# A second level of block products for one of the seven products, in the first feed-forward weights of a streaming encoder layer on one Trainium2 core

## The chip, the cores and the metric

The kernel runs on one core of a Trainium2 chip. The metric is the device time of one execution in microseconds (us), the median of several runs. In the profile the engines are PE (TensorE, matmuls; PEld are its weight loads), DVE (VectorE), ACT (ScalarE), POOL (GpSimd) and SP (SyncE, which only issues transfers; SPq is its queue). All arithmetic is of single precision.

## The reference, cut to what matters

One encoder layer is computed for 1024 new frames and for 64 frames of a second stream, so 1088 rows of 1024 features. It has a half-step feed-forward, attention of two kinds, and a second half-step feed-forward, with a layer norm after each of the three.

```python
def _swiglu(x, wi, wo):
    a, u = jnp.split(x @ wi, 2, axis=-1)
    return (jax.nn.silu(a) * u) @ wo

def _layer(x, mixer, ...):
    h = _layer_norm(alpha * x + 0.5 * _swiglu(x, ffn1_wi, ffn1_wo), ln1_g, ln1_b)
    ...                                  # attention and its projections: mix
    h = _layer_norm(alpha * h + mix, ln2_g, ln2_b)
    h = _layer_norm(alpha * h + 0.5 * _swiglu(h, ffn2_wi, ffn2_wo), ln3_g, ln3_b)
```

`wi` is 1024 x 5632 (a gate half and a linear half of 2816 columns), `wo` is 2816 x 1024. The change concerns `x @ wi` in both feed-forwards.

## The kernel before, in words

**Tiles.** Features lie on the 128 partitions: the residual is eight tiles `y0` to `y7` of 128 features x 1088 columns (`NT`). The 2816 hidden features are 22 tiles (`NF`) of 128, numbered f. A matmul is exact enough only if each factor is split into an upper part (rounded to the format that TensorE takes at full rate) and a lower part (the rest), so each product of 128 x 128 by 128 x 272 (`SUB` = 272, a quarter of the columns) is three matmuls: upper by upper, upper by lower, lower by upper.

**Block products.** With the residual cut into halves of its features and halves of its 1088 columns, A11, A12, A21, A22, a tile's product with `wi` is four blocks by four, and Winograd's scheme makes it from seven block products instead of eight, P1 to P7. Each takes one factor of the residual (A11, A12, A22, or a sum S1 to S4 of blocks, each four row blocks deep) and one block of the weights or a difference of blocks. P1 and P2 are A11 and A12 by the fetched blocks b11 and b21; P6, P5, P3, P7, P4 follow. One product is 2 column parts x 4 row blocks x 3 = 24 matmuls, done by `product`, L921. `after`, L955, moves the results: the first sum of a bank is copied by ACT into a line c (`copy`), later ones are added by DVE (`plus`), then come the silu on ACT and the product of the gate and the linear half on DVE (`times`), whose result is stored in `ff_d` for tiles below 18. There are three lines, c, c21 and c22, used by every tile in turn.

**Order.** `add_ffn7` writes the whole order of a feed-forward (L1371 to 1386): tiles 0 and 1 by plain products (`plain`), tiles 2 and 3 side by side, tiles 4 to 19 singly, one product after the other in the order P1, P2, P6, P5, P3, P7, P4, then tiles 20 and 21 side by side, then the second feed-forward weights. `sums_of_weights`, L1125, stands after P1 of tiles 4 to 12: it fetches four blocks of `wo`, makes four differences of 512 columns on DVE (tiles st) and stores them for later.

**Weights.** Six raw slots of 512 columns (`fetch`, L818; named wr, more and q in the trace) take the fetched blocks. Four slots (w_s) hold a product's split weights. `prepare`, L841, takes the next product's unit when a slot is handed back by `done_with`: a split is one copy of 512 columns on ACT and one difference on DVE; P6 makes four differences of 512 columns first. A planner (`Plan`) places each task in the order of its engine's instructions while the program is written; what engine it is and where it stands is fixed then. In these stages the weights' upper parts are ACT's and the lower parts DVE's, and POOL has nothing to do.

**Around it.** `put_factors`, L715, adds the bias to the normed residual and splits it into A11 to A22 before the second feed-forward. A chain of steps that builds attention bias tables runs beside the first feed-forward's tile loop.

Of the kernel before, what the change touches and what calls it, by code (L numbers as in the profile page):

```python
# [32 lines left out]
P = 128  # L33
# [101 lines left out]
class Plan:  # L135
# [93 lines left out]
    def count(self, e, op, outs, ins, args, kw):  # L229
        dma = op == "dma_start"  # L230
        kept = [x for x in outs if x.space != bass.MemoryType.DRAM or x.tensor.name.startswith(("ff_", "tw_"))]
# [117 lines left out]
def tile_trunk(ctx, tc, a):  # L349
# [34 lines left out]
    o_d = dram.tile([D, NT], F32, name="o_d")  # L384
    bt_d = [dram.tile([P, HEADS * 256], F32, name=f"bt_d{i}") for i in range(2)]
# [329 lines left out]
    def put_factors(G):  # L715

        def put(k, b, y, bias, t0):
            n = TB[b]
            t1 = plan.task(biased(n), f"ln_w{b}", lambda e: plus_bias(e, y[:, :n], bias), [t0], 3)
# [82 lines left out]

    def add_ffn7(wi, wo, wl, G, gi, put, beside_it, last, end):
# [9 lines left out]
        sums_of, made, outs, banks, touched, back = {}, {}, {}, {}, set(), set()  # L813
# [27 lines left out]
        def prepare():  # L841
# [7 lines left out]
            def task(engines, queue, fn, deps, keys=(), reads=()):  # L849
                return plan.task(engines, queue, fn, deps, 1, lambda: all((n, f) in src for n in keys),  # L850
                                 lambda: [x() for x in reads], when)
# [4 lines left out]
            def parts(x, deps, more=(), keys=(), done=None):  # L856
                hi = w[:, 0]

                def copy(e):
                    if e == "act":  # L860
                        nc.scalar.activation(hi, x(), AF.Copy)
                    else:
                        nc.vector.tensor_copy(hi, x())

                def rest(e):
                    of(e).tensor_tensor(w[:, 1], x(), hi.bitcast(F32), op=OP.subtract)
# [3 lines left out]
                t1 = task((("act", 93 + 0.84 * 512), ("dve", WH * (69 + 0.52 * 512)))[alone], "w_h", copy, deps, keys,  # L870
                          [x] if keys else [])
                u.t = low[u.kind, f] = task((("dve", 69 + 1.04 * 512), ("pool", WP * (146 + 2.1 * 512)))[alone], "w_l", rest,
                                            [t1] + list(more))
            if u.kind[0] == "q":
# [5 lines left out]
            elif u.kind == "P6":  # L880
# [3 lines left out]
                m4 = low["t4", f] = task(shared(512), "w_t", minus(b21, b21, b22), [m2, low["P2", f]])  # L884
# [4 lines left out]
            elif u.kind == "P3":  # L889
                parts(part("b22x", f), [], keys=["b22x"], done="b22x")  # L890
            elif u.kind == "P7":
# [29 lines left out]
        def product(f, kind):  # L921
            u = get_unit(kind, f)
            w, factor = u.slot, FACTOR[kind]
            if kind == "P1":
                F[f] = Bag()
                F[f].f, F[f].h, F[f].t, F[f].a, F[f].b = f, G.h(f), {}, {}, {}
            o = F[f]
            h, t = o.h, o.t
            second = f in SECONDS
            base = 4 if second else 0  # L930
            for s in range(2):
                in_b = kind in ("P2", "P7", "P4")
                if kind == "P1":
                    o.a[s] = take_bank(base + s)
                elif kind == "P2":
                    o.b[s] = take_bank(base + 2 + s)
                else:
                    wait(t[{"P6": "r1", "P5": "r2", "P3": "r4", "P7": "c11", "P4": "c22"}[kind], s])
                p = (o.b if in_b else o.a)[s][:, :SUB]
                for k in range(4):  # L940
                    x, c = G.xc[factor][:, k, :, s * SUB:(s + 1) * SUB], slice(k * P, (k + 1) * P)
                    wait(*G.ready[factor, k])
                    first, final = k == 0 and kind in ("P1", "P2", "P7"), k == 3
                    nc.tensor.matmul(p, w[:, 0, c], x[:, 0], start=first, stop=False, skip_group_check=True)
                    nc.tensor.matmul(p, w[:, 0, c], x[:, 1], start=False, stop=False, skip_group_check=True)
                    nc.tensor.matmul(p, w[:, 1, c], x[:, 0], start=False, stop=final, skip_group_check=True)
                    tick()
                if not (second and kind in ("P1", "P2")):
                    after(f, kind, s, p, base)
                if kind == "P7" and f + 1 in SECONDS:  # L950
                    after(f + 1, "P1", s, F[f + 1].a[s][:, :SUB], 4)
                    after(f + 1, "P2", s, F[f + 1].b[s][:, :SUB], 4)
            done_with(u)

        def after(f, kind, s, p, base):  # L955
# [3 lines left out]
            c, c21, c22 = (x[:, s] for x in G.t)  # L959
# [18 lines left out]
            if kind == "P1":  # L978
# [8 lines left out]
            elif kind == "P3":  # L987
# [3 lines left out]
                G.user[0, s] = [t["h1", s]]  # L991
# [10 lines left out]
        def plain(f, half):  # L1002

            if f not in F:
                F[f] = Bag()
                F[f].f, F[f].h, F[f].t = f, G.h(f), {}
# [89 lines left out]
        def early():  # L1096
# [3 lines left out]
            wait(*G.sums_made)  # L1100
            roles.update(mm=[0, 1, 2, 3])
# [274 lines left out]
        for f in range(EIGHT + 2, NF - 2):  # L1376
# [11 lines left out]
        for x, fs in order:  # L1388
            for f in fs:
                if x == "plain":  # L1390
# [4 lines left out]
                    steps.append(lambda f=f, half=half: plain(f, half))  # L1395
                elif x == "beside":
# [41 lines left out]
    HT, SUB = NT // 2, NT // 4  # L1438
    EIGHT = 2
# [12 lines left out]
    G1.y = [yp.tile([P, NT], F32, name=f"y{d}") for d in range(KT)]  # L1452
# [94 lines left out]
    def bias_tables():  # L1547
# [7 lines left out]
        for i in range(2):  # L1555
# [13 lines left out]
            for h in range(HEADS):  # L1569
# [4 lines left out]
                yield later("pe", 9000)  # L1574
# [17 lines left out]
    def after_plain1(f, half):  # L1592
# [7 lines left out]
        if (f, half) == (1, 1):  # L1600
            for _, third in G1.made:
                third()

    G1.after_plain = after_plain1
# [873 lines left out]
    def to_out():  # L2478
# [5 lines left out]
        G2.y = [yp.tile([P, NT], F32, name=f"y2_{d}") for d in range(KT)]  # L2484
# [57 lines left out]
    def after_plain2(f, half):  # L2542
# [9 lines left out]
        if (f, half) == (1, 1):  # L2552
            for _, third in G2.made:
                third()

# [13 lines left out]
    G2.to_second = to_second2  # L2569
# [147 lines left out]
```

## Time and profile before

| | us |
|---|---|
| median of 3 runs | 2436.49 (2435.34 to 2437.27) |
| the profiled execution's own time | 2433.65 |
| its span in the trace | 2431.9 |
| tile loop of pairs, first feed-forward | about 98.6 to 445.7 |
| tile loop of pairs, second feed-forward | about 1795.4 to 2130.9 |

The profile is one page of one execution and a trace that can be queried. A row of the page's fifth part, and of the view by groups, names line, engine, operation, result<-operands and shapes, and then the busy time, the mean duration in ns of one, and the idle time of that engine just before, with what ended it. The helper that records operations makes nearly every row's line L124, so the names tell operations apart: b is a bank of sums, w_s the split weights, wr, more and q the raw weights, A and S the factors, c a line. The table by windows gives for each stretch its length, the busy time (and number of instructions) of PE, PEld, DVE, ACT and POOL, the clock that TensorE was granted, the share of the DMA engines and GB/s. A row of the waits gives engine and what it waited for, the total in us, the number of waits and the longest. A row of the timeline gives start, duration, engine, operation and, in brackets, the idle time before it and what ended that.

### The profile page before, as it was taken

Reading aid. Unit: us, or ns where it says so; the run is one execution under the profiler, and the core shown is the slowest. Engines: PE = TensorE matmul, PEld = TensorE weight load, DVE = VectorE, ACT = ScalarE, POOL = GpSimd, SP = SyncE. Lnnn points to the kernel's source line nnn. Section 1 sums busy time; section 2 is a strip of 40 time slices with the busy share of each in tenths; the row PEclk is TensorE's granted clock in tenths of the full one; section 3 lists DMA queues with packets and bytes.
Section 4 is the critical chain, followed back from the end, with each engine's and each line's share of the span. In section 5 each row is a group of like instructions: output and inputs, shape, how many; then the busy total and the mean of one; then the engine's idle time right before and its main releaser. Section 6 shows DMA issues by size and latency. Waiting matters only on the chain.

```text
span 2431.9 us, 46878 instructions
## 1 busy us (share of the span) xinstructions
PE 2406.8 (99%) x17339; PEld 2363.8 (97%) x17340; DVE 1744.2 (72%) x4248; ACT 1307.8 (54%) x2771; POOL 312.3 (13%) x443
## 2 busy tenths in 40 slices
PE   9999999999999999999999999999999999999998
PEld 9999999999999999999999999999999999999997
DVE  7666655667876889898776677669956665576786
ACT  6333333344435698788866777445643333443344
POOL 0000000000014223222253342211000000000000
PEclk9999999999999999999999999999999999999999
DMA  5476532264223322223221112565256653236323
GB/s 189 128 212 203 175 103 88 66 215 144 85 88 114 119 80 75 93 79 93 85 82 57 57 42 73 172 195 173 82 149 186 188 155 93 80 103 211 109 83 100
DMA packets 228213, 293.29 MB, mean 121 GB/s; under 512 B 21056, under 2 KB 151472, under 8 KB 227952
## 3 DMA queue, kind: packets, MB, share of 16 engines
q1 hardware_dynamic: 221936, 283.38, 37.8%
q10 hardware_dynamic: 5488, 4.70, 0.8%
q8 instruction: 136, 2.23, 0.4%
q0 software_dynamic: 560, 2.21, 0.2%
q14 instruction: 93, 0.76, 0.1%
HBM read 215.48 MB, written 75.00 MB: 119 GB/s over the span
## 4 chain that ended last, share of the span: by engine, by line
PE 86%; DVE 7%; ACT 2%; DMA 2%; issue 1%; SPq 0%; POOL 0%; DVEq 0%; ACTq 0%; POOLq 0%
PE b L124 86%; DVE w L124 1%; DVE y L124 1%; DVE scores L124 1%; ACT scores L124 1%; SPq L124 0%; DVE w_s L124 0%; DVE pt L124 0%; DMA st<-in_wo_dram 0%; ACT w L124 0%; DVE k L124 0%; DVE sc L124 0%; ACT w_s L124 0%; DVE junk L124 0%; DMA x<-o_d 0%
## 5 line engine op out<-in xcount | busy, mean ns | idle before, releaser
L124 PE MATMUL b<-x,w_s 128*128 128x384 f32 (+1 forms) x3528 | 636.3, 332 | 3.4 <-ACT w_s L124 2.5
L124 PE MATMUL b<-A,w_s 128*128 128x272 f32 (+2 forms) x4848 | 634.4, 290 | 3.2 <-ACT rstd L124 0.9
L124 PEld LDWEIGHTS b<-A,w_s 128*128 128x128 f32 x4848 | 619.4, 188 | 7.9 <-DVE A L124 1.6
L124 PEld LDWEIGHTS b<-x,w_s 128*128 128x128 f32 x3528 | 584.8, 188 | 10.8 <-ACT w_s L124 3.2
L124 PE MATMUL b<-S,w_s 128*128 128x272 f32 x4032 | 516.0, 288 | 2.2 <-ACT c L124 2.2
L124 PEld LDWEIGHTS b<-S,w_s 128*128 128x128 f32 x4032 | 508.2, 188 | 5.2 <-ACT c L124 3.5
L124 ACT ACTIVATE w_s<-wr 128x512 fp32r<-128x512 f32 (+1 forms) x373 | 252.4, 678 | 368.4 <-PE b L124 201.6
L124 DVE TENSOR_TENSOR w_s<-wr,w_s 128x512 fp32r<-128x512 f32 (+1 forms) x347 | 252.4, 729 | 138.6 <-ACT w_s L124 135.1
L124 PE MATMUL b<-fac,w_s 128*128 128x272 f32 x1800 | 229.3, 288 | 0.5 <-ACT room L124 0.5
L124 PEld LDWEIGHTS b<-fac,w_s 128*128 128x128 f32 x1800 | 227.1, 188 | 0.8 <-ACT room L124 0.8
L124 POOL TENSOR_TENSOR w_s<-wr,w_s 128x256 fp32r<-128x256 f32 x180 | 139.8, 803 | 304.8 <-ACT w_s L124 124.8
L124 ACT ACTIVATE c<-b 128x272 f32<-128x272 f32 x258 | 100.0, 389 | 90.4 <-PE b L124 83.5
L124 DVE TENSOR_TENSOR c<-c,b 128x272 f32<-128x272 f32 x240 | 103.8, 434 | 61.3 <-PE b L124 58.4
L124 DVE TENSOR_TENSOR pt<-b,pt 128x512 fp32r<-128x512 f32 (+4 forms) x184 | 96.0, 544 | 30.3 <-ACT pt L124 29.1
L124 ACT ACTIVATE c<-c 128x272 f32<-128x272 f32 x160 | 68.9, 432 | 77.1 <-DVE c L124 74.7
L124 ACT ACTIVATE w<-w,mx 128x640 f32<-128x640 f32 (+5 forms) x144 | 100.5, 699 | 12.1 <-DVE mx L124 10.9
L124 ACT ACTIVATE w<-w,sm 128x640 f32<-128x640 f32 (+5 forms) x144 | 98.3, 700 | 9.6 <-DVE sm L124 8.9
L124 PE MATMUL b<-pt,v 128*128 128x256 f32 (+3 forms) x672 | 99.4, 276 | 3.5 <-DVE pt L124 2.7
L124 PEld LDWEIGHTS b<-pt,v 128*128 128x128 f32 (+1 forms) x672 | 94.7, 188 | 7.7 <-DVE pt L124 3.2
L124 PE MATMUL b<-m,w_s 128*128 128x384 f32 (+1 forms) x576 | 98.1, 330 | 0.3 <-DVE w_s L124 0.3
L124 PEld LDWEIGHTS b<-m,w_s 128*128 128x128 f32 x576 | 95.8, 188 | 1.2 <-DVE w_s L124 0.6
L124 ACT ACTIVATE pt<-b 128x512 fp32r<-128x512 f32 (+4 forms) x184 | 82.9, 478 | 20.1 <-PE b L124 18.5
(286 smaller groups left out, 3033.6 us busy)
## 6 DMA issues: line engine op xcount, KB each, us to landing
wr<-in_wi_dram SPq DMA_DIRECT2D x156, 256.0 KB, 3.2
ff_d<-c SPq DMA_DIRECT2D x144, 136.0 KB, 3.0
a<-ff_d SPq DMA_DIRECT2D x72, 272.0 KB, 3.6
st<-in_wo_dram SPq DMA_DIRECT2D x72, 256.0 KB, 5.2
tw_d<-st SPq DMA_DIRECT2D x72, 256.0 KB, 2.5
wr<-in_wz_dram SPq DMA_DIRECT2D x35, 512.0 KB, 3.8
wr<-tw_d SPq DMA_DIRECT2D x48, 256.0 KB, 2.7
wr<-in_wout_dram SPq DMA_DIRECT2D x24, 512.0 KB, 3.7
```

Of the source, the lines that this page charges most:

```text
L124: r = real(*args, **kw)
```

## The change

For the pairs of tiles (4, 5), (6, 7) to (18, 19) of both feed-forwards, sixteen pairs in all, the two products P2 of a pair are made as one product of twice the width, A12 by [b21 of f, b21 of f+1], by the same scheme once more: seven products of quarter blocks instead of eight, each two row blocks deep, 6 matmuls. Their factors are quarter blocks of A12 (A11, A12 and A22 in the code, blocks of that tile) and four new sums of them, `l2_0` to `l2_3`, which `second_level` makes once per feed-forward after the plain tiles. `joint` writes these seven between the products P1, P6 and P5 of f; banks 4 (x below) and 5 (y) take their sums, ACT copies from x to the lines and DVE adds from y; the second tile g = f+1 has a line of its own, `c2`. Three new weight units, Lb, Ld and Lc, take b21 of g, and differences of 256 columns (`temp`) of both b21.

The new tiles lie in the memory of the residual: `l2_0` to `l2_3` in y0 to y3, `temp` in y4, `c2` in y5. These six are loaded again after the last joint (`come_back`): in the first feed-forward from the input, in the second from a new DRAM tile `h2_d`, into which `put_factors` stores them.

The sums of the second feed-forward weights now stand after P3 of tiles 4 to 8, 10, 12, 14 and 16. The planner no longer counts earlier writes of `ff_` and `tw_` tiles in DRAM as something that a write follows, and one wait in the chain of the bias tables is 7000 for 9000.

```diff
@@ put_factors
+            def whole(e):
+                plus_bias(e, y[:, :n], bias)
+                if k < AWAY:
+                    nc.sync.dma_start(h2_d[k * P:(k + 1) * P, TO[b]:TO[b] + n], y[:, :n])
+            t1 = plan.task(biased(n), f"ln_w{b}", whole, [t0], 3)
@@ second_level(G), once per feed-forward
+        for k in range(2):
+            (a11, a21), (a12, a22) = ((y[i + k][:, :SUB], y[i + k][:, SUB:HT]) for i in (4, 6))
...
+            m1 = make(s1, a21, a22, OP.add, deps)
+            m3 = make(s3, a11, a21, OP.subtract, deps)
+            m2 = make(s2, s1, a11, OP.subtract, [m1])
+            p2 = parts("S2", k, s2, [m2])
+            m4 = make(s2, a12, s2, OP.subtract, [p2])
+            parts("S1", k, s1, [m2])
+            parts("S3", k, s3, [m3])
+            parts("S4", k, s2, [m4])
@@ prepare
+            elif u.kind == "Lb":
...
+                m1 = sum_of(0, upper(f + 1), upper(f), deps, [("b21", f), ("b21", f + 1)], [upper(f + 1), upper(f)])
+                m2 = sum_of(1, under(f + 1), temp(0), [m1])
+                m3 = sum_of(2, under(f + 1), upper(f + 1), [m2])
+                low["l2", f] = sum_of(3, under(f), temp(1), [m3])
+                parts(lambda: G.temp[:, :2 * HC], [m2])
+            elif u.kind == "Ld":
+                parts(under(f + 1), [], keys=[("b21", f + 1)], n=HC)
...
+            elif u.kind == "Lc":
+                parts(lambda: G.temp[:, 2 * HC:], [low["l2", f]])
@@ come_back, called at the start of each product
+            if away:
+                d, half = away.pop(0)
...
+                nc.sync.dma_start(G.y[d][:, cols], G.source[d * P:(d + 1) * P, cols])
@@ joint(f), g = f + 1
+            u = get_unit("P2", f)
+            part_of(u, 0, "A11", x, True)
+            copy(f, 0, x)
+            part_of(u, 1, "A12", y, True)
+            plus(f, 0, y)
...
+            piece(u1, f, "P1", 0)
+            ub = get_unit("Lb", f)
+            part_of(ub, 1, "S2", x)
+            copy(f, 1, x)
+            piece(u1, f, "P1", 1)
+            part_of(ub, 0, "S1", x)
+            copy(g, 1, x)
...
+            u6 = get_unit("P6", f)
+            piece(u6, f, "P6", 0)
+            ud = get_unit("Ld", f)
+            part_of(ud, 0, "S4", x)
+            copy(g, 0, x)
+            piece(u6, f, "P6", 1)
...
+            uc = get_unit("Lc", f)
+            part_of(uc, 0, "S3", y, True)
+            plus(g, 1, y)
+            piece(u5, f, "P5", 0)
+            part_of(uc, 1, "A22", y)
+            plus(f, 1, y)
+            piece(u5, f, "P5", 1)
...
@@ after: P1 in a pair adds onto the line
+            if kind == "P1" and o.t.get(("l", s)):
+                plus("r1", c, o.t["l", s])
...
@@ the order
-        for f in range(EIGHT + 2, NF - 2):
+        for f in range(EIGHT + 2, NF - 2, 2):
...
-            for x in FACTOR:
-                order.append((x, (f,)))
-                if x == "P1" and f - EIGHT - 2 < PAIRS:
-                    order.append(("sums", (f - EIGHT - 2,)))
+            order.append(("joint", (f,)))
+            for g in (f, f + 1):
+                if g > f:
+                    order += [(x, (g,)) for x in ("P1", "P6", "P5")]
+                order.append(("P3", (g,)))
+                if left_sums and (g == f or f < EIGHT + 6):
+                    order.append(("sums", (left_sums.pop(0),)))
+                order += [(x, (g,)) for x in ("P7", "P4")]
```

**TensorE at tile 6 of the second feed-forward.** A_19463 is A11 and A_19467 A12 before; S_20460 is P6's factor, S_20459 that of P5; w_s are the two tiles that hold the four weight slots. Before:

```order
L124 MATMUL b_21996<-A_19463,w_s_20398 128x272 x12
L124 MATMUL b_22016<-A_19463,w_s_20398 128x272 x12
L124 MATMUL b_22034<-A_19467,w_s_20398 128x272 x12
L124 MATMUL b_22051<-A_19467,w_s_20398 128x272 x12
L124 MATMUL b_21996<-S_20460,w_s_20464 128x272 x12
L124 MATMUL b_22016<-S_20460,w_s_20464 128x272 x12
```

After, A_19568 is A11 and A_19572 is A12; b_22147 is bank x, b_22148 bank y, S_20571 and S_20570 are the factors of P6 and P5:

```order
L124 MATMUL b_22147<-A_19572,w_s_20514 128x272 x6
L124 MATMUL b_22148<-A_19572,w_s_20514 128x272 x6
L124 MATMUL b_22169<-A_19568,w_s_20575 128x272 x12
L124 MATMUL b_22147<-l_1_21330,w_s_20514 128x272 x6
L124 MATMUL b_22195<-A_19568,w_s_20575 128x272 x12
L124 MATMUL b_22147<-l_0_21336,w_s_20514 128x272 x6
L124 MATMUL b_22169<-S_20571,w_s_20575 128x272 x12
L124 MATMUL b_22147<-l_3_21363,w_s_20514 128x272 x6
L124 MATMUL b_22195<-S_20571,w_s_20575 128x272 x12
L124 MATMUL b_22148<-l_2_21342,w_s_20575 128x272 x6
L124 MATMUL b_22169<-S_20570,w_s_20514 128x272 x12
L124 MATMUL b_22148<-A_19572,w_s_20575 128x272 x6
```

P6 (the factor S_20460 before, S_20571 after) began 48 matmuls behind the tile's start and still does, but the 48 are now P2 for both column parts of one block (12), P1 (24) and two of the quarter-block products (12), and the seven products of the pair's two P2 stand through to P5.

**VectorE at the same place**, from the joint's first add in its line (bank b_22148) to the lower part of P6's weights; wr and more are raw weights, temp the 256-column differences, st a difference of the second feed-forward weights, b_22169 and b_22195 P1's two banks. After:

```order
L124 TENSOR_TENSOR c<-c,b_22148 128x272
L124 TENSOR_TENSOR temp<-more,temp 128x256
L124 TENSOR_TENSOR wr<-wr 128x512
L124 TENSOR_TENSOR c<-c,b_22169 128x272
L124 TENSOR_TENSOR wr<-wr 128x512
L124 TENSOR_TENSOR st_20938<-st_20938,st_20939 128x512
L124 TENSOR_TENSOR wr<-wr 128x512
L124 TENSOR_TENSOR c<-c,b_22195 128x272
L124 TENSOR_TENSOR more<-more,wr 128x512
L124 TENSOR_TENSOR w_s_20575<-wr,w_s_20575 128x512
```

Before, P6's four differences of a tile stood among the adds of the tile ahead (P7's and P4's banks), and the st differences behind P1; now the four (wr three times, more) stand among the adds of the tile's own joint, with one st difference between them.

**SyncE at the start of the second feed-forward**: the last load of the old residual (h), and the first fetch of weights (more). Before:

```order
L124 DMA h_20315<-h_d 128x320 [waits DMAHW6_49]
L124 DMA more<-in_wi_dram 128x512
L124 DMA more<-in_wi_dram 128x512 [waits DMAHW0_49]
```

After (the h_d that is written is `h2_d`):

```order
L124 DMA h_20426<-h_d 128x320 [waits DMAHW0_49]
L124 DMA h_d<-y_0_19560 128x384 [waits Activation_49]
L124 DMA h_d<-y_1_19561 128x384 [waits DMAHW2_49,Activation_49]
L124 DMA h_d<-y_2_19562 128x384 [waits Activation_49]
L124 DMA h_d<-y_3_19563 128x384 [waits DMAHW4_49,Activation_49]
L124 DMA h_d<-y_4_19564 128x384 [waits DMAHW5_49,Activation_49]
L124 DMA more<-in_wi_dram 128x512 [waits DMAHW6_49]
```

The first fetch of weights now stands behind five stores of the residual's second column part, each of which waits for ScalarE's bias.

More of the change, by code (lines that the diff above doesn't have):

```diff
@@ L384, in tile_trunk @@
     o_d = dram.tile([D, NT], F32, name="o_d")
+    h2_d = dram.tile([D, NT], F32, name="h2_d")
     bt_d = [dram.tile([P, HEADS * 256], F32, name=f"bt_d{i}") for i in range(2)]
@@ L849, in task @@
             def task(engines, queue, fn, deps, keys=(), reads=()):
-                return plan.task(engines, queue, fn, deps, 1, lambda: all((n, f) in src for n in keys),
+                keys = [n if isinstance(n, tuple) else (n, f) for n in keys]
+                return plan.task(engines, queue, fn, deps, 1, lambda: all(n in src for n in keys),
                                  lambda: [x() for x in reads], when)
@@ L919, in take_bank, with new @@
             return psp.tile([P, 512], F32, name=f"b{t}", tag=f"b{t}")
[L921 to L928, printed above, removed]
+        def new(f, c, i):
+            o = F[f] = Bag()
+            o.f, o.h, o.t, o.a, o.b, o.c, o.ci = f, G.h(f), {}, {}, {}, c, i
@@ L929, in product, with piece @@
+        def piece(u, f, kind, s):
+            w, factor, o = u.slot, FACTOR[kind], F[f]
+            t = o.t
             second = f in SECONDS
             base = 4 if second else 0
-            for s in range(2):
[L932 to L946, printed above, removed]
-                    tick()
[L948 to L952, printed above, removed]
@@ L953, in product @@
-            done_with(u)
+            in_b = kind in ("P2", "P7", "P4")
+            if kind == "P1":
+                o.a[s] = take_bank(base + s)
+            elif kind == "P2" or kind == "P7" and s not in o.b:
+                o.b[s] = take_bank(base + 2 + s)
+            if kind not in ("P1", "P2"):
+                wait(t[{"P6": "r1", "P5": "r2", "P3": "r4", "P7": "c11", "P4": "c22"}[kind], s])
+            p = (o.b if in_b else o.a)[s][:, :SUB]
+            for k in range(4):
+                x, c = G.xc[factor][:, k, :, s * SUB:(s + 1) * SUB], slice(k * P, (k + 1) * P)
+                wait(*G.ready[factor, k])
+                first, final = k == 0 and kind in ("P1", "P2", "P7"), k == 3
+                nc.tensor.matmul(p, w[:, 0, c], x[:, 0], start=first, stop=False, skip_group_check=True)
+                nc.tensor.matmul(p, w[:, 0, c], x[:, 1], start=False, stop=False, skip_group_check=True)
+                nc.tensor.matmul(p, w[:, 1, c], x[:, 0], start=False, stop=final, skip_group_check=True)
+                tick()
@@ new lines, in piece, with product @@
+            if not (second and kind in ("P1", "P2")):
+                after(f, kind, s, p, base)
+            if kind == "P7" and f + 1 in SECONDS:
+                after(f + 1, "P1", s, F[f + 1].a[s][:, :SUB], 4)
+                after(f + 1, "P2", s, F[f + 1].b[s][:, :SUB], 4)
+        def product(f, kind):
+            come_back()
+            u = get_unit(kind, f)
+            if kind == "P1" and f not in F:
+                new(f, G.t[0], 0)
+            for s in range(2):
+                piece(u, f, kind, s)
+            done_with(u)
@@ L1100, in early @@
             wait(*G.sums_made)
+            assert not away
+            Y.update({(d, b): G.y[d][:, to[b]:to[b] + tb[b]] for d in range(AWAY) for b in range(3)})
             roles.update(mm=[0, 1, 2, 3])
@@ L1451, in tile_trunk @@
     yp = pool(open_("keep1"), "y")
-    G1.y = [yp.tile([P, NT], F32, name=f"y{d}") for d in range(KT)]
+    G1.yp = yp
+    G1.y = [yp.tile([P, NT], F32, name=f"y{d}", tag=f"y{d}") for d in range(KT)]
     rp = pool(open_("ring1"), "ring1")
```

144 lines of the change are left out of this document (126 added, 18 removed).

## The prediction

> **What bounds the kernel now.** I read the page's first part, its chain and the long groups first, then the table by windows inside the changed stage, then the waits, and last the timeline of single hand-overs.
>
> ```profile
> PE 2406.8 (99%) x17339; PEld 2363.8 (97%) x17340; DVE 1744.2 (72%) x4248; ACT 1307.8 (54%) x2771; POOL 312.3 (13%) x443
> PE 86%; DVE 7%; ACT 2%; DMA 2%; issue 1%; SPq 0%; POOL 0%; DVEq 0%; ACTq 0%; POOLq 0%
> 1860.00:1920.00 60.00, 60.00 (x484) 60.00 (x483) 38.38 (x70) 22.69 (x48) 0.00 (x0) 1.00 0.65 198
> 1980.00:2040.00 60.00, 60.00 (x484) 60.00 (x483) 32.37 (x61) 23.89 (x50) 0.00 (x0) 1.00 0.32 90
> PE b L124 <- ACT c L124: 0.8, 2, 0.4
> PE b L124 <- ACT c L124: 0.6, 2, 0.4
> ```
>
> TensorE is busy for 99% of the span and carries 86% of the chain. In both windows of 60 us inside the second feed-forward's tile loop it is never idle, at a granted clock of 1.00: 60 us by 484 matmuls is **124.0 ns per 128x272 matmul**. VectorE is busy for 38.4 and 32.4 us of 60 there, ScalarE for 22.7 and 23.9. The last two rows are all that TensorE's matmuls waited for ScalarE between 1740 and 2160 us and between 120 and 480 us: two waits each. So every matmul taken out is worth its 124 ns, unless something that now has slack stops TensorE instead.
>
> **The matmuls.** A pair of tiles has two P2 products, 2 x 24 = 48 matmuls. Seven quarter-block products of 2 row blocks and 3 matmuls each make 42. Six fewer, 8 pairs, two feed-forwards: 96 fewer, by 0.1240 us = **-11.90 us**, half in each feed-forward. TensorE's rows show exactly this and nothing else: 480 fewer from A, 384 more from the second-level factors, all 128x272. The products come in groups of 6 where there were 12. I take the same rate: the stage already mixes groups of 3, 12 and 24 from different factors, and the two windows give the same count.
>
> **What a missed hand-over costs.** This is the price of all the rest; the trace has two, both on ScalarE, at tile 3's P5 and P6:
>
> ```profile
> 1779.07 3.17 PE L124 MATMUL b<-S,w_s 128*128 128x272 f32 x24
> 1782.60 1.76 PE L124 MATMUL b<-S,w_s 128*128 128x272 f32 x12 [0.36 <-ACT c L124]
> 1784.79 7.76 PE L124 MATMUL b<-S,w_s 128*128 128x272 f32 x60 [0.43 <-ACT c L124]
> 1792.38 9.14 PE L124 MATMUL b<-A,w_s 128*128 128x272 f32 x72
> 1782.15 0.40 ACT L124 ACTIVATE c<-b 128x272 f32<-128x272 f32 x1 [1.98 <-PE b L124]
> 1784.34 0.69 ACT L124 ACTIVATE c<-b 128x272 f32<-128x272 f32 x2 [1.27 <-DMA ff_d<-c]
> ff_d<-c SPq DMA_DIRECT2D x144, 136.0 KB, 3.0
> ```
>
> From 1779.07 to 1792.38 run 24 + 12 + 60 = 96 matmuls in 13.31 us, where 96 x 0.124 = 11.90 would do. 1.41 us is lost in two stalls, **0.7 us each** (the wait that the profile names, 0.36 and 0.43, is the smaller part). ScalarE copied bank to c late, the second time since the store of the old c to ff_d, 3.0 us long, had not landed.
>
> **How fast VectorE goes through its queue** decides whether the new order makes such stalls:
>
> ```profile
> 336.26 0.43 DVE L124 TENSOR_TENSOR c<-c,b 128x272 f32<-128x272 f32 x1
> 336.61 0.68 DVE L124 TENSOR_TENSOR wr<-wr,q 128x512 f32<-128x512 f32 x1
> 337.33 0.69 DVE L124 TENSOR_TENSOR wr<-wr 128x512 f32<-128x512 f32 x1
> 337.94 0.43 DVE L124 TENSOR_TENSOR c<-c,b 128x272 f32<-128x272 f32 x1
> 338.28 0.68 DVE L124 TENSOR_TENSOR w_s<-wr,w_s 128x512 fp32r<-128x512 f32 x1
> 334.58 0.44 DVE L124 TENSOR_TENSOR c<-c,b 128x272 f32<-128x272 f32 x1 [0.23 <-PE b L124]
> L124 ACT ACTIVATE w_s<-wr 128x512 fp32r<-128x512 f32 x96 | 60.4, 631 | 120.4 <-PE b L124 44.5 <-DVE wr L124 43.9 <-issue 25.2
> L124 DVE TENSOR_TENSOR w_s<-wr,w_s 128x512 fp32r<-128x512 f32 x97 | 66.6, 690 | 53.7 <-ACT w_s L124 52.9
> ```
>
> The operation behind a 272-column add starts 0.35 us after it (336.26 to 336.61), behind a 512-column one 0.61 (337.33 to 337.94), or 0.72 where it reads that one's result (336.61 to 337.33). A waiting add starts 0.23 us after TensorE's last matmul. ScalarE splits off a block's upper part in 0.63 us, VectorE its lower part in 0.69; a product's third matmul needs the lower part.
>
> The Trainium skill's page "VectorE: DVE Perf Modes", section "The DRAIN you can't avoid", says that the next operation does not start until the pipe is empty, and one that isn't held starts earlier. These rows show the second, also for an add that carries a wait; were each held for its whole duration, the sum below would lose 4.4 us more (the second rival).
>
> **P6's weights.** P6 takes four differences of fetched weights and a split. There are four weight slots, and a slot's preparation is written down when the fourth unit before it is done. Before, the three units between were P4, P1 and P2 of 24 matmuls each: 72 x 0.124 = 8.93 us from slot to use. Now they are P2 (12), P1 (24), Lb (12): 48 matmuls, 5.95 us, and its third matmul at 6.20. In a plain joint VectorE passes the adds and differences in 4.7 us by the spacings above, so 1.5 us are left. In the second and third joint (tiles 6 and 8) of each feed-forward the differences of the second feed-forward weights (st) now stand between. Walking the rows of tile 6 in the section on the change: the line's first add at 1.72 us (12 matmuls and 0.23), temp 2.07, wr 2.41, P1's first add 3.21, wr 3.56, st 4.17, wr 4.78, P1's second add 5.44, the last difference 5.79, the lower part 6.40 to 7.09. The upper part ends at 6.14, 0.24 late; the lower part reaches TensorE at 7.14 instead of 6.44. That is 0.95 us lost in each of the second feed-forward's two; in the first one's, where the upper part is in time, 6.65 instead of 6.20, so 0.45. Together 2 x 0.95 + 2 x 0.45 = **+2.8 us**; between 0, if one add less falls in the way, and 5.6, one and four tenths each, with whole durations.
>
> **The hand-overs in the line.** Bank x is used four times in a row and copied by ScalarE before S1 (ready 4.9, wanted 5.21 us from the joint's start), before S4 (7.1, 7.44) and VectorE's add to g's line before A22 (11.6, 11.9). Each is on time by about 0.3 us only, after 12 matmuls (1.49 us) for start (0.23), operation (0.4) and queue. No such margin is in the trace. Nothing lost is one end, one missed hand-over of 0.7 in each of the twelve plain joints the other, 8.4. I take the near end, 0.05 each, **+0.6**, since a step of 12 matmuls is 1.49 us and start and copy need 0.63.
>
> **The start of the second feed-forward.** SyncE now issues five stores of h2 ahead of the first weights, and each waits for the bias of its y on ScalarE:
>
> ```profile
> 1688.79 0.91 SPq L124 DMA_DIRECT2D more<-in_wi_dram  x2
> 1695.79 0.60 ACT L124 ACTIVATE y<-y,lnp 128x384 f32<-128x384 f32 x1
> 1696.88 1.15 ACT L124 ACTIVATE w_s<-more 128x512 fp32r<-128x512 f32 x2
> 1700.20 0.54 PE L124 MATMUL b<-A,w_s 128*128 128x272 f32 x3
> 1701.82 0.81 PE L124 MATMUL b<-c,ones 128*128 128x320 f32 x2 [1.08 <-DVE c L124]
> more<-in_wi_dram SPq DMA_DIRECT2D x37, 256.0 KB, 3.2
> ```
>
> The fifth bias is that of 1695.79, done at 1696.39. The fetch moves from 1688.79 to about 1696.8, lands 3.2 us later at 1700.0; upper part 1700.7, lower part 1701.85 at VectorE's queue there. TensorE's first three matmuls, at 1700.20 now, thus finish about 1.4 to 1.6 us later. But the mean of the layer norm (ones) now stands behind 21 of the product's matmuls, not 3, so its wait of 1.08 goes. Net **+0.5**, between -1.1 (the transfer is in time, the wait gone) and +3.2 (one landing in full).
>
> **What I cost at nothing, and its cover.** The second level's factors: per feed-forward 8 sums and 8 lower parts of 272 columns, 16 x 0.35 = 5.6 us of VectorE, and 8 copies (3.1 us) of ScalarE, while tiles 2 and 3 run for 41.7 us.
>
> ```profile
> 1760.00:1770.00 10.00, 10.00 (x82) 10.00 (x81) 6.27 (x12) 4.72 (x10) 0.00 (x0) 1.00 0.36 111
> 1770.00:1780.00 10.00, 10.00 (x82) 10.00 (x81) 7.10 (x15) 4.95 (x11) 0.00 (x0) 1.00 0.34 105
> 1780.00:1790.00 10.00, 9.21 (x71) 8.77 (x71) 3.14 (x6) 2.90 (x8) 0.00 (x0) 1.00 0.42 119
> 1790.00:1800.00 10.00, 10.00 (x83) 10.00 (x82) 7.41 (x15) 3.87 (x8) 0.00 (x0) 1.00 0.33 88
> ```
>
> VectorE is idle for 16.1 us of these 40. Without that cover the first joint would wait up to 5.6 us, once per feed-forward. In each pair VectorE gets 3.8 us more (three adds, four 256-column differences, the split of one block), 9% of 41.7, from 54 to 64% up to 63 to 75%; ScalarE some 1 us. The y reloads, 12 of 272 KB per feed-forward, and 18 stores of h2 run where the DMA engines' share is 0.32. Uncovered, one fetch behind them would cost TensorE up to its 3.2 us.
>
> **Sum** against the profiled execution's own time, 2433.65: -11.90 + 2.8 + 0.6 + 0.5 = -8.0, or 2425.65. The median of the runs, 2436.49, is 2.84 above that execution; with it, **2428.5 us**.
>
> **The rivals.**
> - *No new waits.* The spacings leave the sums' joints in time, and the start is even: -11.9, 2424.6. For it: four of 16 joints carry all my P6 term, by under 1 us each.
> - *The waits eat the gain.* Two mechanisms. If VectorE held each operation for its whole 0.43 or 0.69, the sums' joints lose 1.4 twice and 1.0 twice and the add before A22 comes 0.25 late in twelve: 4.8 + 3.0 + 0.5, net -3.6, 2432.9. If one hand-over per joint is missed at 0.7, 16 x 0.7 = 11.2 and 0.5 more: 2436.3. For it: three margins of 0.3 in a row. Against both: no such stall in the single products of now, and for the first, 336.26 to 336.61.
> - *Slower: bank x on ScalarE.* Its queue is served in order, and the splits of 0.63 us stand between the four copies of x. If a split comes before the copy, the copy is 0.6 late against a margin of 0.3, and TensorE stops twice per joint: 2 x 0.7 x 16 = 22.4, net +10.5, **2447**. It decides from 11.9 / 16 = 0.74 us per joint. For it: both stalls of the trace are just this, a copy to c too late. Against: ScalarE is busy for 38% only (22.69 of 60), and the margins above already count the splits that the order puts ahead of each copy.
> - *That it doesn't do what it says*, six matmuls costing twelve's time: TensorE's 484 per window in each mix speak against it; part of the second rival.
>
> **Chances.** Forecast, 2426.5 to 2431.5: 0.50. No new waits: 0.17. Waits eat it, 2431.6 to 2437: 0.22, of which 0.05 for a VectorE that holds each operation. Slower: 0.11. The range, 2424 to 2437, leaves out about the last and a little. About 0.2% (4.9 us) is what a measurement of this kernel can tell from no change: the first two are faster (0.67), the third the same (0.22), the last slower (0.11).
>
> **What would show it.** Right: 96 matmuls fewer; TensorE's waits in the joints of tiles 6 and 8 before P6, on w_s, 0.5 to 1 us, and none in joints 10 to 18; the first weight fetch of the second feed-forward some 8 us later than now against the biases of y, and TensorE's wait for ones gone. Wrong: waits on c from ScalarE before S1 or S4 in every joint; waits before A22 on VectorE; windows of the joints with under 484 matmuls per 60 us; a wait for l2 before the first joint; a wait for y at the end.

## The result, and the profile after

The changed kernel took **2463.6 us** (median of 5 runs, 2457.7 to 2466.2) where the kernel before took 2436.25 in runs beside it: ratio 1.0111, 95% interval 1.0095 to 1.0126, so 27 us slower. The forecast was 2428.5 with a range of 2424 to 2437. It was outside on the far side, and beyond the slower rival (2447) too. On another chip the same kernel gave 2457.9 against 2435.9 (1.0093, 1.0079 to 1.0107). Of all runs below one, of e6, took 12384 us at a granted clock of 0.177, and it is left out of that ratio.

First the page of the changed kernel: busy time by engine, and the chain that ended last, by engine and by line.

```profile
PE 2407.4 (98%) x17244; PEld 2358.1 (96%) x17244; DVE 1799.2 (73%) x4421; ACT 1319.3 (54%) x2820; POOL 314.7 (13%) x445
PE 79%; DVE 11%; DMA 5%; issue 2%; ACT 1%; SPq 1%; POOL 0%; DVEq 0%; ACTq 0%
PE b L124 79%; DMA st<-in_wo_dram 4%; DVE c L124 2%; DVE st L124 2%; DVE w_s L124 1%; SPq L124 1%; DVE y L124 1%; DVE wr L124 0%; DMA ff_d<-c 0%; DMA y<-in_xT_dram 0%; DVE scores L124 0%; DVE sc L124 0%; DMA g<-g_d 0%; DVE w L124 0%; DVE lns L124 0%
```

The chain of the kernel before, by line, was this:

```profile
PE b L124 86%; DVE w L124 1%; DVE y L124 1%; DVE scores L124 1%; ACT scores L124 1%; SPq L124 0%; DVE w_s L124 0%; DVE pt L124 0%; DMA st<-in_wo_dram 0%; ACT w L124 0%; DVE k L124 0%; DVE sc L124 0%; ACT w_s L124 0%; DVE junk L124 0%; DMA x<-o_d 0%
```

TensorE's share of the chain fell from 86 to 79%. What grew is a transfer that rounded to 0% before and now has 4%: st<-in_wo_dram, the loads of `wo` blocks for the differences of the second feed-forward weights. Those differences (DVE st, 2%) and the additions to the lines (DVE c, 2%) came in with it. Then the same two windows as before, in the second feed-forward's tile loop:

```profile
1860.00:1920.00 60.00, 56.06 (x431) 54.12 (x430) 40.40 (x79) 24.05 (x53) 0.00 (x0) 1.00 0.51 162
1980.00:2040.00 60.00, 58.77 (x467) 58.36 (x466) 39.71 (x81) 22.88 (x50) 0.00 (x0) 1.00 0.36 114
```

431 and 467 matmuls where there were 484, at an unchanged clock of 1.00. VectorE is busy for 40.4 and 39.7 us of 60: it is not full. Now the waits, of the changed kernel first from 120 to 480 us and then from 1740 to 2190 us (total us, times, longest):

```profile
DVE st L124 <- DMA st<-in_wo_dram: 19.3, 16, 3.2
PE b L124 <- DVE c L124: 13.2, 11, 2.1
DVE st L124 <- DMA st<-in_wo_dram: 14.5, 15, 2.0
PE b L124 <- DVE c L124: 9.7, 9, 1.7
```

and of the kernel before, from 120 to 480 and from 1740 to 2160:

```profile
DVE st L124 <- DMA st<-in_wo_dram: 12.9, 13, 2.1
DVE st L124 <- DMA st<-in_wo_dram: 19.1, 18, 2.4
```

This pair of views carries the case. VectorE waited for these loads before the change as well, 12.9 and 19.1 us in all, about as long as now. But then no TensorE wait stood behind it; now there are 20 waits of TensorE for an addition that VectorE makes. One place in the timeline of the changed kernel shows how (queue of SyncE, then VectorE, then TensorE):

```profile
1964.07 2.14 SPq L124 DMA_DIRECT2D st<-in_wo_dram  x4
1968.04 0.69 DVE L124 TENSOR_TENSOR st<-st,st 128x512 f32<-128x512 f32 x1 [0.41 <-DMA st<-in_wo_dram]
1968.64 0.43 DVE L124 TENSOR_TENSOR c<-c,b 128x272 f32<-128x272 f32 x1
1968.99 0.69 DVE L124 TENSOR_TENSOR w_s<-wr,w_s 128x512 fp32r<-128x512 f32 x1
1971.18 0.69 DVE L124 TENSOR_TENSOR st<-st,st 128x512 f32<-128x512 f32 x1 [1.50 <-DMA st<-in_wo_dram]
1971.79 0.43 DVE L124 TENSOR_TENSOR c<-c,b 128x272 f32<-128x272 f32 x1
1973.09 0.43 DVE L124 TENSOR_TENSOR c<-c,b 128x272 f32<-128x272 f32 x1
1974.99 0.79 DVE L124 TENSOR_TENSOR c<-c,b 128x272 f32<-128x272 f32 x2
1967.52 6.39 PE L124 MATMUL b<-A,w_s 128*128 128x272 f32 x48
1975.58 4.64 PE L124 MATMUL b<-S,w_s 128*128 128x272 f32 x35 [1.67 <-DVE c L124]
```

The four loads are issued behind P3, from 1964.07 on. What one takes is in the view of transfers (KB each, median us from issue to landing):

```profile
st<-in_wo_dram SPq DMA_DIRECT2D x72, 256.0 KB, 4.5
```

VectorE's second difference waits for the last of them until 1971.18, and everything behind it in VectorE's queue is late: the two additions of P4 (1971.79, 1973.09), and then P1's two (1974.99). P1's first product had ended 36 matmuls after 1967.52, at 1972.0; its addition ran 3 us later, and P6 of g, which stands only 12 matmuls behind, waited. From 1967.52, 48 matmuls by 0.124 us end at 1973.47; P6 began at 1975.58, so 2.11 us were lost. In the kernel before, the same step stands behind P1, and the same differences wait as long (VectorE):

```profile
1971.09 0.69 DVE L124 TENSOR_TENSOR st<-st,st 128x512 f32<-128x512 f32 x1 [1.39 <-DMA st<-in_wo_dram]
1971.70 0.68 DVE L124 TENSOR_TENSOR w_s<-more,w_s 128x512 fp32r<-128x512 f32 x1
1973.12 2.15 DVE L124 TENSOR_TENSOR st<-st,st 128x512 f32<-128x512 f32 x3 [0.74 <-DMA st<-in_wo_dram]
1975.18 1.29 DVE L124 TENSOR_TENSOR w_s<-wr,w_s 128x512 fp32r<-128x512 f32 x2
```

There they fall into P6 and P5, whose results ScalarE copies: no addition for TensorE stands in the queue behind them.

For the sum I count **gaps**: a TensorE row's start in the timeline, less that of the row before it, less the matmuls of the row before by 0.124 us, where this is over 0.25 us and the row before is of 128x272 matmuls, from 60 to 510 us and from 1680 to 2200 us (the timeline asked for in stretches of 30 us). Before: 3.3 and 2.9 us. After: 25.3 and 23.2. The 42 us more, less the 11.9 that the matmuls saved, make 30; the two profiled executions lie 32.3 apart (2433.65 and 2465.97).

Of the 48.5 us after, 29.0 stand at rows whose named wait is for an addition by VectorE (DVE c). Two gaps in the first feed-forward, 1.69 us before 198.00 and 1.75 before 276.34, name no wait at all. There the clock that TensorE was granted was half for a while (table by windows, 16 and 15 matmuls in 3.3 us):

```profile
192.10:195.40 3.30, 3.30 (x16) 3.30 (x16) 3.01 (x9) 1.06 (x2) 0.00 (x0) 0.50 0.41 150
270.60:273.90 3.30, 3.30 (x15) 3.30 (x16) 0.79 (x2) 1.45 (x4) 0.00 (x0) 0.50 0.62 185
```

Each of these stretches begins as TensorE resumes behind a gap that an addition made, of 2.25 us (to 191.85) and of 2.41 (to 270.50). That the gap brought the lower clock on is likely and not shown: gaps of 2.11 us, to 124.13 and to 1975.58, were not followed by one.

### The profile page after: what moved, and what is told of

Same layout as the page of the kernel before. It is cut to its first block, busy times and chain, and to the rows that moved or that the text cites. A ratio compares the mean times of both kernels' runs of the same rounds, so it can differ in the third digit from the quotient of the medians.

```text
span 2464.2 us, 46933 instructions
## 1 busy us (share of the span) xinstructions
PE 2407.4 (98%) x17244; PEld 2358.1 (96%) x17244; DVE 1799.2 (73%) x4421; ACT 1319.3 (54%) x2820; POOL 314.7 (13%) x445
## 4 chain that ended last, share of the span: by engine, by line
PE 79%; DVE 11%; DMA 5%; issue 2%; ACT 1%; SPq 1%; POOL 0%; DVEq 0%; ACTq 0%
PE b L124 79%; DMA st<-in_wo_dram 4%; DVE c L124 2%; DVE st L124 2%; DVE w_s L124 1%; SPq L124 1%; DVE y L124 1%; DVE wr L124 0%; DMA ff_d<-c 0%; DMA y<-in_xT_dram 0%; DVE scores L124 0%; DVE sc L124 0%; DMA g<-g_d 0%; DVE w L124 0%; DVE lns L124 0%
## 5 line engine op out<-in xcount | busy, mean ns | idle before, releaser
L124 PE MATMUL b<-A,w_s 128*128 128x272 f32 (+3 forms) x4368 | 586.4, 292 | 14.0 <-DVE c L124 8.3
L124 PEld LDWEIGHTS b<-A,w_s 128*128 128x128 f32 x4368 | 565.1, 189 | 21.2 <-DVE c L124 11.4
L124 PE MATMUL b<-S,w_s 128*128 128x272 f32 x4032 | 528.1, 289 | 21.5 <-DVE c L124 14.7
L124 ACT ACTIVATE w_s<-wr 128x512 fp32r<-128x512 f32 (+2 forms) x367 | 245.0, 670 | 269.5 <-PE b L124 165.4
L124 DVE TENSOR_TENSOR w_s<-wr,w_s 128x512 fp32r<-128x512 f32 (+2 forms) x341 | 244.7, 720 | 131.1 <-ACT w_s L124 126.1
L124 DVE TENSOR_TENSOR c<-c,b 128x272 f32<-128x272 f32 x288 | 123.3, 434 | 48.4 <-PE b L124 43.8
```

Source lines behind the costliest of these rows:

```text
L124: r = real(*args, **kw)
```

## The experiments

**e1: the differences later, nothing else.** The step stays behind P3; the planner may place its differences only 6 us after its own estimate of the landing.

```diff
+            landed = plan.dma + 300 + 6000
...
-                last = [plan.task(shared(512), "w_x", go, last, 6, None, [r[x], r[y]])]
+                last = [plan.task(shared(512), "w_x", go, last, 6, None, [r[x], r[y]], 0.0, lambda: landed)]
```

> The changed kernel, in which only the four differences of wo blocks (st) of each sums step may be placed later: not before 6 us after the planner's own estimate of their loads' landing. Everything else, the joints too, is as it was. Theory 1 (the differences stand in VectorE's queue ahead of the adds from banks, and hold them until the loads have landed): the waits of TensorE for c from VectorE before the second half of P4 and before P6 of g go, which add up to about 29 us by gaps; 2463.6 - 29 gives 2433 to 2438, and some 10 us at P6 of f in the joints of tiles 6 and 8 and around the second level stay. Rival (VectorE is simply too full in the pairs, or each add in its place is late by its own chain): the waits stay, 2455 to 2466.

Measured 2424.2 us (2423.4 to 2426.4), before beside it 2434.1; ratio 0.996 (0.9946 to 0.9975). Faster than theory 1 had it, since the gaps at the joints of tiles 6 and 8 went too. In the table by windows of e1, TensorE is never idle in either window, with VectorE busier than in the changed kernel; of the gaps that are left, 1.5 and 5.3 us in the two ranges, none lies in a joint, and 1.6 of the 5.3 fall in a stretch at half the clock (0.52 from 1694.90 to 1698.10 us).

```profile
1860.00:1920.00 60.00, 60.00 (x483) 60.00 (x483) 45.41 (x87) 23.78 (x53) 0.00 (x0) 1.00 0.53 170
1980.00:2040.00 60.00, 60.00 (x483) 60.00 (x482) 41.86 (x82) 23.60 (x51) 0.00 (x0) 1.00 0.44 143
```

The rival, a VectorE that is too full, falls: it is busier here and stops nobody. The shorter wait in the chain of the bias tables (7000 for 9000) is in this kernel too, so it isn't the loss; it was not tried alone.

**e2: the steps back behind P1** (of g), except for two of nine per feed-forward.

```diff
-                    order += [(x, (g,)) for x in ("P1", "P6", "P5")]
+                    order.append(("P1", (g,)))
+                    if left_sums:
+                        order.append(("sums", (left_sums.pop(0),)))
+                    order += [(x, (g,)) for x in ("P6", "P5")]
                 order.append(("P3", (g,)))
-                if left_sums and (g == f or f < EIGHT + 6):
+                if left_sums and g > f and f < EIGHT + 6:
```

> The changed kernel with seven of the nine sums steps of each feed-forward moved from behind P3 to behind P1 of the second tile g (as far from P7, P4 and P1 as before the change); two stay behind P3 of g, in the first two pairs. Theory 1: 14 of 18 places of the wait go, 2463.6 - 14/18 x 29 = 2441, and since the joints of tiles 6 and 8 then have no st differences at their front, part of their 10 us goes too: 2434 to 2442. Rival (VectorE too full): no less than 2455.

Measured 2444.9 us (ratio 1.004, 1.0024 to 1.0055), somewhat above what was expected. The gaps are 13.8 and 13.2 us, and apart from tiles 2 and 3, the start and one of 0.26 us they lie at the four steps left behind P3 and in the joints after them. Among them 3.3 us in the first feed-forward, and 1.65 at the start of the second, are gaps without a named wait, in stretches at a granted clock of 0.50 to 0.53. The largest (TensorE, P4's second half):

```profile
192.84 6.30 PE L124 MATMUL b<-A,w_s 128*128 128x272 f32 x36 [3.81 <-DVE c L124]
```

**e3 and e12: the planner's count as before.**

```diff
-        kept = [x for x in outs if x.space != bass.MemoryType.DRAM]
+        kept = [x for x in outs if x.space != bass.MemoryType.DRAM or x.tensor.name.startswith(("ff_", "tw_"))]
```

> The changed kernel with the planner's count of DRAM writes as it was before (ff_ and tw_ tiles are followed again). Theory 2 (the loads come later than planned because the planner no longer counts what the stores wait for, so it places the differences too early): the waits go, 2435 to 2442. Theory 1 (it is the place behind P3, and the planner's view of the landing is too early with either count): within 4 us of the changed kernel, 2459 to 2467.

Measured 2457.4 us (ratio 1.0099, 1.0082 to 1.0115), just under theory 1's range and far above theory 2's. That is 6 us under the changed kernel, but the two were on different chips, so both ran again side by side, as e11 and e12:

> The changed kernel unaltered, beside e12 on one chip, since e3 and the result came from different chips and their intervals overlap (1.0082 to 1.0115 and 1.0095 to 1.0126). Both theories: ratio near 1.011, 2460 to 2466 if the kernel before is at 2435.

> e3 once more, on the chip of e11. If the planner's count is no part of the loss, within 2 us of e11; if it is a small part, 4 to 7 us less than e11, all of it in the first feed-forward's tile loop (by gaps, e3 lost 18.8 us there and the changed kernel 25.3, while in the second they lost 24.7 and 23.2).

The changed kernel gave 2457.9 (ratio 1.0093, 1.0079 to 1.0107), with the old count 2460.1 (1.0097, 1.0082 to 1.0112). The count is no part of the loss that these runs can tell. The changed kernel itself differs as much: its gaps in the first feed-forward were 25.3 us in one execution and 19.8 in e11's, of the same program. 3.4 of these 5.5 us are the two stretches at half the clock, which e11 has nowhere in its first feed-forward.

**e4: the place alone**, in the kernel before, without joints.

```diff
-                if x == "P1" and f - EIGHT - 2 < PAIRS:
-                    order.append(("sums", (f - EIGHT - 2,)))
+                if x == "P3" and f in (4, 5, 6, 7, 8, 10, 12, 14, 16):
+                    order.append(("sums", ((4, 5, 6, 7, 8, 10, 12, 14, 16).index(f),)))
```

> The kernel before, no joints, with the sums steps behind P3 of tiles 4 to 8, 10, 12, 14 and 16, where the change puts them. Theory 1 in its plain form (the place alone makes the stall: P7's add, 12 matmuls ahead of P4's second use of the bank, waits behind an st difference): some 0.7 to 1.5 us at each of 18 places, 2449 to 2463. Rival (the place harms only where the next hand-over is one of the new tight ones, P1 of g to P6 of g over 12 matmuls, and l): 2435 to 2440.

Measured 2462.5 us (ratio 1.0117, 1.0102 to 1.0132): the edit of the place costs 28 us, with no joint in the program. The gaps are 25.1 and 8.4 us. Not all are the theory's: 12.9 us of them stand at waits for an addition by VectorE in the two tile loops, and the longest is a different load:

```profile
120.44 0.69 DVE L124 TENSOR_TENSOR st<-st,st 128x512 f32<-128x512 f32 x1 [4.16 <-DMA st<-in_wo_dram]
121.05 0.43 DVE L124 TENSOR_TENSOR c<-c,b 128x272 f32<-128x272 f32 x1
423.83 1.19 PE L124 MATMUL b<-one,flip 128*128 128x256 f32 x2 [6.42 <-DMA one<-row_d]
```

The first two rows are the theory: an addition of P7 behind a difference that waited 4.16 us. The third is the chain of the bias tables: TensorE came to its step in the new order before that step's load had landed. Its 6.4 us are not the sums' wait, and why it came out so was not tried. So e4 shows that the place alone makes such waits, but not that it makes 28 us of them. In the second feed-forward the place costs 5.5 us here (8.4 less 2.9), and the change cost 20 (23.2 less 2.9). A part of the difference is P1 of g: the change makes its results additions of VectorE, and 7 of the 9 waits for additions in the changed kernel's second loop, 10.1 us of gaps, stand before P6 of g, 12 matmuls behind. e4 has none there.

**e5: 3 us in place of 6** (the edit of e1 with 3000).

> As e1, but the differences only 3 us behind the planner's estimate of the landing. Theory 1 with the size of the planner's error: VectorE's waits for these loads were 3.2 us at most in the changed kernel, so 3 us should take nearly all away: 2424 to 2429. If it is not the wait for the loads but where the differences stand among the adds (any place near them costs), part of the loss stays: 2432 to 2450.

2425.5 us (ratio 0.997, 0.9959 to 0.9981). 3 us are enough, as the longest wait of 3.2 us said. This run also parts the wait from the place. Differences stand right ahead of both of P1's additions of g here, none of them waits, and P6 of g begins on time, 48 matmuls behind TensorE's row of 1975.34 (VectorE, then TensorE):

```profile
1980.09 0.68 DVE L124 TENSOR_TENSOR st<-st,st 128x512 f32<-128x512 f32 x1
1980.69 0.43 DVE L124 TENSOR_TENSOR c<-c,b 128x272 f32<-128x272 f32 x1
1981.04 0.68 DVE L124 TENSOR_TENSOR st<-st,st 128x512 f32<-128x512 f32 x1
1981.64 0.43 DVE L124 TENSOR_TENSOR c<-c,b 128x272 f32<-128x272 f32 x1
1975.34 6.15 PE L124 MATMUL b<-A,w_s 128*128 128x272 f32 x48
1981.33 8.90 PE L124 MATMUL b<-S,w_s 128*128 128x272 f32 x70
```

So a difference of 0.7 us among these additions does no harm; one that waits does.

**e6: the edit of e1 in the kernel before.**

> The kernel before, with the one edit of e1 (the differences not before 6 us after their loads' estimated landing) and no other. Theory: in the kernel before the waits for the loads cost TensorE nothing (its gaps in the two loops, 3.3 and 2.9 us, are at copies by ScalarE), so 2431 to 2437, and the joints themselves are worth e1 against this, about 10 us. Rival: the late place alone is what made e1 fast: 2424 to 2428 here.

2434.2 us, ratio 0.9997 (0.9987 to 1.0007). No change, so e1's gain is the joints' own.

**e7: e1, with the second level's factors later**, behind P5 of tile 3.

```diff
                     steps.append(lambda f=f, x=x: product(f, x))
+                    if (x, f) == ("P5", EIGHT + 1):
+                        steps.append(lambda: second_level(G))
```

(and its two calls behind the plain tiles taken out)

> As e1, with the second level's factors made behind P5 of tile 3 instead of behind the plain tiles. Theory: e1's remaining gaps, 3.2 us at tiles 2 and 3 of the second feed-forward where the kernel before has 1.3, come from the factors' eight copies on ScalarE standing there: they fall to about 1.3, so 1 to 2 us less than e1, 2421 to 2424. Rival: the gaps are the old ones (the store of the line to ff_d), no change, 2424; and if 8.9 us do not suffice for the factors, the first joint waits, 2426 or more.

2420.0 us (2416.9 to 2421.8), ratio 0.9945 (0.993 to 0.9959): **the fastest version, 13.9 us under the kernel before**, though the interval overlaps e1's (0.9946 to 0.9975). The gaps at tiles 2 and 3 of the second feed-forward fell from 3.2 to 0.95 us. The first joint does not wait.

**e8: e7, with h2 stored later**, in six transfers behind the plain tiles.

```diff
-                if k < AWAY:
-                    nc.sync.dma_start(h2_d[k * P:(k + 1) * P, TO[b]:TO[b] + n], y[:, :n])
@@ behind the plain tiles
+            for k in range(AWAY):
+                nc.sync.dma_start(h2_d[k * P:(k + 1) * P, :], G2.y[k][:, :])
```

> As e7, with the residual's h2 copies stored in six transfers behind the plain tiles instead of eighteen out of the bias steps, so that the first weights of the second feed-forward are fetched as early as before the change. Theory of the prediction (the start costs 0.5 us, between -1.1 and 3.2): 0.5 to 1.8 us less than e7, since e1 waits 1.8 us there for the weights. Rival (the wait for the norm's mean takes its place): no less than 0.5.

2422.8 us (ratio 0.9957, 0.9943 to 0.9972): nothing gained, where 0.5 to 1.8 us were expected. The start of the second feed-forward in e1, with the early stores (two rows), and then two rows of e8 (TensorE); e7, which e8 changes, has the waits of e1's rows at 0.75 and 0.88:

```profile
1694.43 0.52 PE L124 MATMUL b<-A,w_s 128*128 128x272 f32 x2 [1.61 <-ACT w_s L124]
1695.15 4.12 PE L124 MATMUL b<-A,w_s 128*128 128x272 f32 x19 [0.21 <-DVE w_s L124]
1695.62 0.81 PE L124 MATMUL b<-c,ones 128*128 128x320 f32 x2 [1.08 <-DVE c L124]
1758.55 0.52 PE L124 MATMUL b<-S,w_s 128*128 128x272 f32 x2 [0.76 <-ACT w_s L124]
```

e8's weights are in time, but the wait for the mean (1.08, as before the change) is back, and a new wait for weights came 63 us later; what delayed these was not tried.

**e9: the loads one step earlier.** The step stays behind P3, but its loads are issued at the step before.

```diff
+            if j + 1 < PAIRS:
+                load_weights(j + 1)
```

(`load_weights` holds the four loads; the first step still issues its own)

> The changed kernel with the sums steps where the change puts them, behind P3, but the four loads of each step issued one step earlier (at the step before it, into the other set of st tiles), so that the differences still stand among the adds of P7, P4 and P1 and no longer wait for their loads. Theory 1 (it is the wait for the loads that holds the adds behind it): as e1, 2423 to 2430. Rival (the 0.7 us of each difference ahead of an add with a margin of a few tenths is enough): at 18 steps some 0.7 to 1.4 us each stay, 2437 to 2450. The gaps at P6 of f in the joints of tiles 6 and 8 tell how much of them is occupation alone.

2431.2 us (ratio 0.9986, 0.9977 to 0.9995), a little above theory 1. VectorE's waits for the loads fell from 19.3 to 1.5 us in the first feed-forward and TensorE's for additions from 13.2 to 0.8. These are the two rows of e9, from 120 to 480 us:

```profile
DVE st L124 <- DMA st<-in_wo_dram: 1.5, 2, 0.8
PE b L124 <- DVE c L124: 0.8, 2, 0.6
```

In the second feed-forward's loop, 3.0 of its 3.5 us of gaps lie at the first step, whose loads are not early; behind the other eight steps there is a single one, of 0.6 us. e9 is not the changed kernel's order less the wait, though. The planner counts with the earlier landing and places the differences of these eight steps between P3's and P7's additions; none is left ahead of P4's or P1's, or among P6's own, where the expectation had them. What parts wait and place is e5.

**e10: e9 and e7 together.**

> As e9, with the second level's factors made behind P5 of tile 3 as in e7. If e9 is as fast as e1, this is as fast as e7: 2418 to 2423. If e9 keeps a loss, this keeps it, less some 3 us.

2427.6 us (ratio 0.9969, 0.9956 to 0.9981): it keeps e9's loss at the first step and is 3.5 us under e9, as the second case had it.

## Why the prediction was wrong

**The step that failed** is "The hand-overs in the line", with the term of P6 beside it. Both walked VectorE's queue with each operation's duration and spacing. They took it that an operation starts when its turn comes. And the list of hand-overs has no term for P1's additions of g before P6 of g, where most is lost in the second loop (10.1 us by gaps). The differences st were counted once, at P6 of tiles 6 and 8, as 0.6 us each, and nowhere else. But the change moved the whole step, its four loads included, from behind P1 to behind P3, and a difference can't start until its loads have landed, 4.5 us after issue in the changed kernel. 12 and 24 matmuls behind P3's end come P7's additions, then P4's, then P1's of g; what stands behind the difference waits with it. Of the 42 us of new gaps only those at P6, 4.5 us in four joints, had a term in the sum. The row that warned of it is VectorE's 19.1 us of waits for these loads before the change. It was left out of the sum, since it cost TensorE nothing then; that was true of its place and not of the wait. The runs take the wait away in three ways (e1 and e5; e2 for most steps; e9), and the time follows each time; e5 keeps differences ahead of P1's additions and loses nothing; e4 makes such waits without the joints. The prediction's own sign of being wrong came: windows of the tile loop with 431 and 467 matmuls where 484 were expected.

By its other steps:

- *The matmuls, -11.9 us.* Borne out. With the wait gone (e1) the kernel is 9.9 us faster than before, between 6 and 13 by its interval, and the same edit without joints (e6) gives nothing. 483 matmuls in each full window say that groups of 6 run at the rate of groups of 12.
- *P6's weights, +2.8.* The sign came true, TensorE's waits for w_s before P6 at tiles 6 and 8, but not for the reason given. The changed kernel has these waits in the second feed-forward's joint of tile 6 (TensorE), with three rows of VectorE before them:

```profile
1864.44 0.52 PE L124 MATMUL b<-S,w_s 128*128 128x272 f32 x2 [0.75 <-ACT w_s L124]
1865.28 1.51 PE L124 MATMUL b<-S,w_s 128*128 128x272 f32 x10 [0.32 <-DVE w_s L124]
1856.60 0.69 DVE L124 TENSOR_TENSOR st<-st,st 128x512 f32<-128x512 f32 x1 [0.81 <-DMA st<-in_wo_dram]
1860.14 0.43 DVE L124 TENSOR_TENSOR c<-c,b 128x272 f32<-128x272 f32 x1
1864.53 0.69 DVE L124 TENSOR_TENSOR w_s<-wr,w_s 128x512 fp32r<-128x512 f32 x1
```

  The named waits, 1.07 us together, lie near the 0.95 forecast, but by gaps 1.63 us were lost (1.04 and 0.59), and 4.5 in the four joints where 2.8 were forecast. The walk from the line's first addition to the end of the lower part took 5.08 us (1860.14 to 1865.22), where 5.37 were forecast, so the spacings held. But the walk began late: the joint starts at 1856.39 (24 matmuls and a gap of 0.37 before TensorE's row at 1859.74), and the addition came 3.75 us behind that, not 1.72. VectorE had stood before it for the loads, 1.39 us (to 1853.95) and 0.81. That the waits fell on the joints named is in part luck. In e5 two differences that don't wait stand in the same stretch (1833.06 and 1835.92 us at tile 6), behind the first two of P6's four own differences (1831.51 and 1832.46). There, and in e1, where none stands so, P6 does not wait in any of the 16 joints. So the differences' durations alone cost nothing in the order that e5 has; in the changed kernel's order, no run shows what they would.
- *The tight hand-overs, +0.6.* In e1 there is no gap over 0.25 us at any copy or addition of a joint: margins of 0.3 us hold if the queue ahead does not stop. Zero.
- *The start of the second feed-forward, +0.5.* e1 waits 1.61 + 0.21 = 1.82 us there by name, where 1.08 was: +0.7. Half a clock then costs e1 1.6 us more, behind these waits; the changed kernel, with 1.56 and 0.21, keeps the full clock there. As said, the wait for the mean is what it trades against, which e8 shows from the other side.
- *The second level at nothing.* Not quite: its copies cost ScalarE's hand-overs at tiles 2 and 3 about 2 us in the second feed-forward (3.2 us of gaps against 1.3), which e7 took back.
- *VectorE's share*, forecast at 63 to 75% (64 and 9 make 73), is 70 and 76% in e1's windows.
- *A VectorE that holds each operation.* Not seen: in the timeline above, the operation behind an addition of 0.43 us starts 0.35 later (1968.64 to 1968.99), and the addition behind a difference of 0.69 starts 0.61 later (1971.18 to 1971.79).
- *Slower by bank x on ScalarE.* Not the cause. Among its joints, the changed kernel has waits for ScalarE's copies only in those of tiles 6 and 8, 2.8 us of gaps in all, and e1 has none. Without the term of P6, which e1 takes away, the sum forecasts 10.8 us saved, and e1 saved 9.9: nearly all that failed is the one wait.

## What to carry to other kernels

When a change moves a step that begins with loads, ask at its new place what stands in the engine's queue behind the first operation that reads them, and put the loads' landing time, not the operation's duration, against the room there. A wait that costs nothing in the waits view is harmless only where it is. Two cheap cures worked here: tell the planner that the loads land later (3 us was enough), or issue them one step earlier.

## What the hardware showed

A stall of TensorE costs more than the wait that the profile names: at 1975.58 us it names 1.67 and 2.11 us were lost, and in the changed kernel's second range the gaps exceed the named waits by 0.17 to 0.58 us each. A stall can also be followed by a stretch at a granted clock of 0.50, for some 3.4 us in the two places of the changed kernel, which cost 1.7 us each, in rows that name no wait. Two profiles of this one program differ by it: 25.3 and 19.8 us of gaps in the first feed-forward, of which these two stretches are 3.4.
